# Key projections from high and low halves, mixtures without differences, and first users of loads placed later, in a hybrid convolution and RWKV-7 step

## The chip, the cores and the metric

The kernel runs on one core of one Trainium2 chip. The time is the device time of one execution in microseconds (us). Five engines work side by side and meet at semaphores: TensorE (PE in the profile; PEld is its loading of weights), VectorE (DVE), ScalarE (ACT), GpSimd (POOL) and SyncE (SP), which here issues loads. Each engine takes its instructions in the order in which they were queued: while the one at the head waits, those behind it wait too. A reader follows a wait from the engine that idles to the instruction that released it.

## What is computed

One inference step through two layers in single precision: a causal convolution layer with its MLP, then an RWKV-7 layer with its MLP, on 1040 prompt tokens (16 of them learned) and 8 decode tokens, model width 1024, 16 heads of 64. The change lies in the RWKV-7 layer:

```python
    prev = jnp.concatenate([shift_prev[:, None, :].astype(h.dtype), h[:, :-1]], axis=1)
    xx = prev - h
    xr = h + xx * x_mix[0]
    xw = h + xx * x_mix[1]
    xk = h + xx * x_mix[2]
    xv = h + xx * x_mix[3]
    xa = h + xx * x_mix[4]
    xg = h + xx * x_mix[5]
    r = (xr @ w_r).astype(f32)
    k = (xk @ w_k).astype(f32)
    v = (xv @ w_v).astype(f32)
    ...
    kk = kk / jnp.maximum(jnp.sqrt(jnp.sum(kk * kk, axis=-1, keepdims=True)), L2_EPS)
    k = k * (1.0 + (a - 1.0) * k_a.astype(f32))
    ...
    S_final, ys = lax.scan(_wkv7_step, S0.astype(f32), xs)
```

Each token is mixed with the one before it (`x_mix`), and six mixtures are projected. `_wkv7_step` is the recurrence over tokens; the kernel does it in chunks of 64 tokens, which needs the inverse of a small triangular matrix for each chunk and head.

## The kernel before

Activations lie with the model's 1024 rows as 8 tiles of 128 partitions, tokens along the free axis. The convolution layer and both MLPs go in three groups of about 350 tokens. Their products are made of halves: ScalarE rounds a weight block to the fast format (`wo_hi`, L158), GpSimd subtracts to get the rest (`wo_lo`, L165), the activations are split alike (`split`, L141 and L142), and `mm3` (L190 to L192) issues three products, high x high, low weight x high, high weight x low. A product in full precision is one call that leaves two records on TensorE.

The RWKV-7 mixer takes its 1048 tokens in four groups, counted from 0, of 272, 256, 256 and 264 columns (`mixer_in`). Each group runs a loop over p = 0 to 7, the output tiles of 128 rows. A step p projects r (`proj`, L909), then the gate and the two small matrices for decay and rate (l_g, l_w, l_a), then v, then the products for the step before (vt, nn, nm, the head sum pk at L1078), then pb (L803), which spreads the keys' norm. The key projections run one group ahead: those of group 0 stand before its loop, and the blocks of group g+1 stand at the end of the steps of group g (block p-1 in step p, and block 7 also in step 7). All r, k and v products are in full precision. Their weights come through one stream of loads (`col_stream`) into five buffers, four blocks ahead.

`prepare(g)` makes the mixtures: VectorE and GpSimd subtract (`xx`, L873), VectorE multiplies and adds (`mix`, L883). Index 2 is the key's mixture, 0 r's, 3 v's, 5 the gate's. In step p=1 the eight key mixtures of the next group are made in a row. Mixtures of the next group's gate and r follow during p=7.

PSUM has four banks in rotation for these products ("mm"), so a product waits until the reader of the fourth product before it is through: the copy of v's product to `vv` (ScalarE, L1114) is such a reader, and so is VectorE's `hl` in the MLP.

Beside this loop the recurrence (A, gg, bT, W, U, S, Y on TensorE) runs chunk by chunk; it is advanced at fill points inside the projections. The inverses (`inverses`) load `ni` and run some 30 pairs of tt and ni on VectorE (L1208, L1209). When the mixer ends, `mixer_out` splits its result into z_h and z_l (L142) and the last MLP begins; during it `decode_step` does the 8 decode tokens: four transposes and writes to memory (`d_dec`, L1426), one load `dq` (L1429) and 16 rounds on VectorE from L1444 on.

TensorE's order is that of the program. VectorE's and ScalarE's order comes from a scheduler that runs a timed model while the program is built; `tc.issue_after(x)` pins an instruction behind x on its engine, `kept_place` keeps it where the program has it, and the numbers that generators yield say how much filling work goes between two pieces. The mask `nmask` (L774) of the inverses' input is made from a loaded mask `m_ar` while the first layer's MLP runs.

Of the kernel before, what the change touches and what calls it, by code (L numbers as in the profile page):

```python
# [16 lines left out]
P = 128  # L17
# [29 lines left out]
def hybrid_step(tc, x_prompt, x_sample, state_conv, state_shift, state_wkv, meta_tokens,  # L47
# [10 lines left out]
    with ctx:  # L58
# [80 lines left out]
        def split(hi, lo, src, eng_lo):  # L139

            nc.scalar.copy(hi, src)  # L141
            return eng_lo.tensor_sub(lo, src, hi.bitcast(F32))  # L142
# [35 lines left out]

        def col_stream(cols, ahead):

            raws = {}
            for i in range(len(cols)):
                for j in range(i, min(i + ahead + 1, len(cols))):
                    if j not in raws:
                        raws[j] = load_raw(col_src(*cols[j][:2]), (KT, P), cols[j][2])
                yield blocks_of(raws.pop(i))
# [135 lines left out]
        def mlp(layer, groups, lag, eng_w, eng_h, fill=None, done=None):  # L322
# [16 lines left out]
            def inp(j, w, group):  # L339
                gn, hv, n, ah, al, rs, hid_pool = group  # L340
                if j % 2 == 0:
                    hid[gn, j // 2] = [hid_pool.tile([P, 2, cur["wide"]], F32R, name=f"h{q}{layer}{gn}_{j}", tag=f"h{q}") for q in "hl"]
                hh, hl = hid[gn, j // 2]
                ps = dense(w, (ah, al), n, f"in{layer}_{j}_{gn}", fill)
                with tc.high_priority(offset=HR):
                    s = ps[:, :n]
                    nc.vector.scalar_tensor_tensor(s, s, 0.0, rs()[:, :n], op0=ALU.max, op1=ALU.mult)  # L347
                    nc.scalar.activation(s, s, AF.Square)  # L348
                    low = split(hh[:, j % 2, :n], hl[:, j % 2, :n], s, eng_h)
                    marks.setdefault(f"hl{gn}", []).append(low.ins)  # L350
# [423 lines left out]
        nc.vector.tensor_scalar(nmask, m_ar[:, :32], par32[:, 0:1], None, op0=ALU.mult)  # L774
# [41 lines left out]

        hnp = pool(ld, "hnp", 1)
        mixp = pool(ld, "mixp", 24)
# [15 lines left out]
        prep, norm, kept, scans = {}, {}, {}, {}  # L834
# [22 lines left out]
        def prepare(g):  # L857
# [12 lines left out]
            xx = hnp.tile([P, KT, N1], F32, name=nm("xx"), tag="xx")  # L870
            for k in range(KT):
                with nullcontext() if g else tc.issue_after(marks["hl2"][k + 5]):
                    first = (nc.gpsimd if k % 3 == 2 else nc.vector).tensor_sub(xx[:, k, :npr], hx[:, k, 0:npr], hx[:, k, 1:1 + npr])  # L873
                if g and k in (0, 2):
                    kept_place(first)
                yield
            if npr < n:
                nc.vector.tensor_sub(xx[:, :, npr:n], sps, hx[:, :, 1 + npr:1 + n])
            def mix(i, k):

                t = mixp.tile([P, N1], F32, name=nm("mx", i, k), tag="mx")
                with nullcontext() if g else tc.issue_after(marks["out2"][2 * (k - KT) + 1 if i == 2 else -1]):
                    nc.vector.scalar_tensor_tensor(t[:, :n], xx[:, k, :n], vec("x_mix", i * KT + k), hx[:, k, 1:1 + n],  # L883
                                                   op0=ALU.mult, op1=ALU.add)
                return t[:, :n]
# [14 lines left out]

        def keys_of(p):
# [11 lines left out]

        def keys(g, fill):
# [4 lines left out]
            act = [mix(2, k) for k in range(KT)]  # L919
# [5 lines left out]
            for p in range(KT):  # L925
                yield
                ps = proj(next(wrkv), act, n, nm("k", p), fill)
# [7 lines left out]
            r16 = lorap.tile([P, N1], F32, name=nm("r16"), tag="lf")  # L935
# [8 lines left out]
        def mixer_in(g, tick):  # L944
# [140 lines left out]
            for p in range(KT):  # L1085
# [23 lines left out]
                for pl, t, nb, sign in zip(pls, (cum, nav), ("w0", "a0"), (0.5, -0.5)):  # L1109
                    nc.scalar.activation(t[:, :n], pl[:, :n], AF.Tanh, scale=0.5, bias=hvec(nb, p))  # L1110
                    nc.scalar.activation(t[:, :n], t[:, :n], AF.Copy, scale=sign, bias=sign)
# [35 lines left out]
                for s in segs:  # L1147
# [6 lines left out]
                    nc.vector.tensor_mul(out(2), two(wa[:, :2, :]), cols(em, s).unsqueeze(2).broadcast_to([P, s[2], 2, s[3]]))  # L1154
# [7 lines left out]
                if g < 3:  # L1162
                    if p == 0:
# [24 lines left out]
        def inverses(c, n):  # L1188
# [8 lines left out]
            group = next((g for g in range(4) if CHUNKS[g][0] > max(c, 1)), None)  # L1197
            while group and group not in scans:
# [4 lines left out]
            for j in range(top - 2, 0, -1):  # L1203
# [3 lines left out]
                with tc.issue_after(scans[group]) if group and j == top - 2 else nullcontext():  # L1207
# [207 lines left out]
        def decode_step():  # L1415

            with ExitStack() as s:
# [12 lines left out]
                yield 6  # L1430
# [149 lines left out]
        with ExitStack() as l1:  # L1580
# [15 lines left out]
            def mixer_out(g, actp, fill, add):  # L1596
# [5 lines left out]
                for p in range(0, KT, per):  # L1602
# [6 lines left out]
                    for i in range(some):  # L1609
                        split(z[0][p + i][:, :n], z[1][p + i][:, :n], v[:, i], nc.vector)  # L1610
# [72 lines left out]
            DL, DN, NL = 74, 90, 16  # L1683
# [75 lines left out]
```

## Time and profile before

| what | us |
|---|---|
| three runs | 2680.71, 2673.79, 2672.78 |
| median | 2673.79 |
| the profiled execution, its own time | 2680.24 |
| its span in the profile | 2678.5 |
| TensorE busy in it | 2602.9 (97%) |
| VectorE, ScalarE, GpSimd busy | 1725.7, 1132.7, 1450.9 |

The profiled execution took 2680.24 us, 1.7 more than the span that the page divides and 6.45 more than the median. A row of a timeline gives the start within the span, the busy time, engine, line, operation, output and inputs, and in brackets how long the engine had idled before it and what ended that. A row with x2 holds several instructions on end. In a row of clock windows stand the stretch, its length, each engine's busy time and count (PE, PEld, DVE, ACT, POOL), TensorE's granted clock as a share of full speed, the share of the DMA engines' time in use, and GB/s. Groups give the count, the total and the mean in ns.

### The profile page before, as it was taken

Reading aid. Unit: us, or ns where it says so; the run is one execution under the profiler, and the core shown is the slowest. Engines: PE = TensorE matmul, PEld = TensorE weight load, DVE = VectorE, ACT = ScalarE, POOL = GpSimd, SP = SyncE. Lnnn points to the kernel's source line nnn. Section 1 sums busy time; section 2 is a strip of 40 time slices with the busy share of each in tenths; the row PEclk is TensorE's granted clock in tenths of the full one; section 3 lists DMA queues with packets and bytes.
Section 4 is the critical chain, followed back from the end, with each engine's and each line's share of the span. In section 5 each row is a group of like instructions: output and inputs, shape, how many; then the busy total and the mean of one; then the engine's idle time right before and its main releaser. Section 6 shows DMA issues by size and latency. Waiting matters only on the chain.

```text
span 2678.5 us, 51360 instructions
## 1 busy us (share of the span) xinstructions
PE 2602.9 (97%) x19796; PEld 2450.6 (91%) x19796; DVE 1725.7 (64%) x3584; ACT 1132.7 (42%) x2097; POOL 1450.9 (54%) x2060
## 2 busy tenths in 40 slices
PE   9999999999999999999899999899999999999998
PEld 8999999999998999877777887689999999999998
DVE  6999999997445444444857567686679643344435
ACT  5546445444444333333344445545443542222223
POOL 7677878878877776122211113375578763333331
PEclk9999999999999999999999999999999999999999
DMA  6663544554456443668766867897666542222211
GB/s 188 176 168 104 167 141 132 158 177 134 142 154 183 124 138 113 201 188 211 188 181 180 206 168 193 209 211 179 156 204 176 155 131 71 64 71 71 67 52 44
DMA packets 602058, 400.20 MB, mean 149 GB/s; under 512 B 96128, under 2 KB 548928, under 8 KB 601814
## 3 DMA queue, kind: packets, MB, share of 16 engines
q1 hardware_dynamic: 573764, 360.08, 49.1%
q0 software_dynamic: 8720, 26.35, 3.1%
q10 hardware_dynamic: 19330, 10.49, 1.4%
q8 instruction: 156, 2.56, 0.4%
q14 instruction: 88, 0.72, 0.1%
HBM read 338.94 MB, written 58.83 MB: 149 GB/s over the span
## 4 chain that ended last, share of the span: by engine, by line
PE 79%; DVE 11%; DMA 3%; ACT 2%; issue 2%; POOL 2%; SPq 0%; ACTq 0%; DVEq 0%; POOLq 0%
PE out L190 8%; PE ps_in L190 8%; PE ps_in L192 8%; PE ps_in L191 8%; PE out L191 8%; PE out L192 8%; PE pk L909 4%; PE pr L909 3%; PE pv L909 2%; DVE tt L1208 1%; DVE ni L1209 1%; PE ps_g L190 1%; PE ps_o L192 1%; PE ps_g L191 1%; PE ps_g L192 1%
## 5 line engine op out<-in xcount | busy, mean ns | idle before, releaser
L165 POOL TENSOR_TENSOR wo_lo<-wo_raw,wo_hi 128x256 fp32r<-128x256 f32 x736 | 539.3, 765 | 290.0 <-ACT wo_hi L158 281.0
L165 POOL TENSOR_TENSOR wi_lo<-wi_raw,wi_hi 128x256 fp32r<-128x256 f32 x640 | 474.7, 774 | 250.5 <-ACT wi_hi L158 249.8
L190 PE MATMUL out<-hh,wo_hi 128*128 128x352 f32 (+2 forms) x1536 | 499.8, 325 | 14.9 <-DVE hl L142 10.2
L360 DVE TENSOR_TENSOR h<-h,out 128x352 f32<-128x352 f32 (+2 forms) x768 | 386.9, 512 | 169.7 <-PE out L192 168.0
L190 PE MATMUL ps_in<-m_h,wi_hi 128*128 128x352 f32 (+2 forms) x1536 | 495.3, 322 | 0.0
L192 PE MATMUL ps_in<-m_l,wi_hi 128*128 128x352 f32 (+2 forms) x1536 | 494.2, 322 | 1.1 <-DVE m_l L288 1.1
L191 PE MATMUL out<-hh,wo_lo 128*128 128x352 f32 (+2 forms) x1536 | 494.5, 322 | 0.0
L191 PE MATMUL ps_in<-m_h,wi_lo 128*128 128x352 f32 (+2 forms) x1536 | 492.9, 321 | 0.0
L192 PE MATMUL out<-hl,wo_hi 128*128 128x352 f32 (+2 forms) x1536 | 492.8, 321 | 0.0
L542 DVE SCALAR_TENSOR_TENSOR cv<-u,wdw,cv 128x348 f32<-128x348 f32 (+2 forms) x720 | 378.4, 577 | 0.7
L158 ACT CAST wi_hi<-wi_raw 128x1024 fp32r<-128x1024 f32 x160 | 167.6, 1049 | 398.1 <-PE out L192 199.0
L158 ACT CAST wo_hi<-wo_raw 128x1024 fp32r<-128x1024 f32 x184 | 192.7, 1048 | 318.3 <-PE out L192 169.9
L190 PEld LDWEIGHTS out<-hh,wo_hi 128*128 128x128 f32 x1536 | 291.0, 189 | 21.1 <-DVE hl L142 11.5
L192 PEld LDWEIGHTS ps_in<-m_l,wi_hi 128*128 128x128 f32 x1536 | 289.2, 188 | 2.6 <-DVE m_l L288 2.1
L190 PEld LDWEIGHTS ps_in<-m_h,wi_hi 128*128 128x128 f32 x1536 | 290.3, 189 | 1.4
L191 PEld LDWEIGHTS out<-hh,wo_lo 128*128 128x128 f32 x1536 | 290.1, 189 | 0.8
L191 PEld LDWEIGHTS ps_in<-m_h,wi_lo 128*128 128x128 f32 x1536 | 289.5, 188 | 0.6
L192 PEld LDWEIGHTS out<-hl,wo_hi 128*128 128x128 f32 x1536 | 289.8, 189 | 0.0
L347 DVE SCALAR_TENSOR_TENSOR ps_in<-ps_in,rs_m 128x352 f32<-128x352 f32 (+2 forms) x192 | 100.6, 525 | 258.1 <-PE ps_in L192 257.8
L142 DVE TENSOR_TENSOR hl<-ps_in,hh 128x352 fp32r<-128x352 f32 (+2 forms) x192 | 98.7, 515 | 125.2 <-ACT hh L141 125.2
L1074 POOL DMA_DIRECT2D d_n<-n x32 | 24.3, 760 | 217.5 <-DVE n L1064 112.4
L348 ACT ACTIVATE ps_in<-ps_in 128x352 f32<-128x352 f32 (+2 forms) x192 | 85.1, 444 | 125.2 <-DVE ps_in L347 124.8
(367 smaller groups left out, 4770.1 us busy)
## 6 DMA issues: line engine op xcount, KB each, us to landing
wi_raw<-in_w_mlp_in_dram SPq DMA_DIRECT2D x160, 512.0 KB
wo_raw<-in_w_mlp_out_dram SPq DMA_DIRECT2D x160, 512.0 KB
wk_raw<-in_rwkv_w_k_dram SPq DMA_DIRECT2D x32, 512.0 KB
wr_raw<-in_rwkv_w_r_dram SPq DMA_DIRECT2D x32, 512.0 KB
wv_raw<-in_rwkv_w_v_dram SPq DMA_DIRECT2D x32, 512.0 KB
d_ab<-ab POOLq DMA_DIRECT2D x32, 512.0 KB, 4.5
pg_raw<-in_conv_w_pw_dram SPq DMA_DIRECT2D x24, 512.0 KB
pa_raw<-in_conv_w_pw_dram SPq DMA_DIRECT2D x24, 512.0 KB
```

Of the source, the lines that this page charges most:

```text
L142: return eng_lo.tensor_sub(lo, src, hi.bitcast(F32))
L158: cast = nc.scalar.copy(hi[:, :a * b], raw[:, :a * b])
L165: eng_lo.tensor_sub(lo[:, cs], raw[:, cs], hi[:, cs].bitcast(F32))
L190: nc.tensor.matmul(ps, w[0], act[0], start=first, stop=False)
L191: nc.tensor.matmul(ps, w[1], act[0], start=False, stop=False)
L192: nc.tensor.matmul(ps, w[0], act[1], start=False, stop=last)
L347: nc.vector.scalar_tensor_tensor(s, s, 0.0, rs()[:, :n], op0=ALU.max, op1=ALU.mult)
L348: nc.scalar.activation(s, s, AF.Square)
L360: total = nc.vector.tensor_add(hv[:, 4 * i + m, :], hv[:, 4 * i + m, :], ps[:, :n])
L542: nc.vector.scalar_tensor_tensor(acc[m][:, :n], ug[:, m, j:j + n], wdw[:, m, j:j + 1], acc[m][:, :n], op0=ALU.mult, op1=ALU.add)
L909: nc.tensor.matmul(ps[:, :n], w[:, k, :], act[k], start=k == 0, stop=k == KT - 1)
L1208: nc.vector.tensor_mul(o, ni[:, :j, j:j + 1].broadcast_to([B, j, wd]), ni[:, j:j + 1, j + 1:top].broadcast_to([B, j, wd]))
```

## The change

1. The key projections of groups 1 to 3 become three products of halves (`proj_split`). The key mixtures are split in `halved` (ScalarE rounds, VectorE subtracts), the weight blocks in `split_block` (the same engines, 128x1024 elements). The high and low weights take two further buffers of the same five, and the stream loads three blocks ahead.
2. A mixture is x_previous * m by ScalarE, then x * (1 - m) + that by VectorE (`omix` holds 1 - m). The differences xx are gone, and so are eight of the 24 buffers.
3. The key mixtures are made after the rates of step p=1, pinned on ScalarE behind `rate` and on VectorE behind the last product of step 0 (`decayed`). `nmask` is pinned behind a later split of the MLP, the last inverses' first tt behind the last z_l, and the decode step's wait count and start (6 to 12, 90 to 96) move.
4. `em` takes the place of `cum` and is computed after the other exponentials.

```diff
+                        if cols[j][3]:
+                            halves.append((raw, *(cur["raw"].tile([P, 8 * P], F32R, name=f"{cols[j][2]}_{q}", tag="raw") for q in "hl")))
...
-        nc.vector.tensor_scalar(nmask, m_ar[:, :32], par32[:, 0:1], None, op0=ALU.mult)
+        with tc.issue_after(marks["hl2"][14]):
+            nc.vector.tensor_scalar(nmask, m_ar[:, :32], par32[:, 0:1], None, op0=ALU.mult)
...
-        mixp = pool(ld, "mixp", 24)
+        mixp = pool(ld, "mixp", 16)
+        khl = pool(ld, "khl", 1)
...
-            for k in range(KT):
-                with nullcontext() if g else tc.issue_after(marks["hl2"][k + 5]):
-                    first = (nc.gpsimd if k % 3 == 2 else nc.vector).tensor_sub(xx[:, k, :npr], hx[:, k, 0:npr], hx[:, k, 1:1 + npr])
...
+                with tc.issue_after(a_pin) if a_pin else nullcontext():
+                    nc.scalar.activation(t[:, :npr], hx[:, k, 0:npr], AF.Copy, scale=m)
...
+                with tc.issue_after(v_pin) if v_pin else nullcontext():
+                    nc.vector.scalar_tensor_tensor(t[:, :n], hx[:, k, 1:1 + n], omix[:, i * KT + k:i * KT + k + 1], t[:, :n],
                                                    op0=ALU.mult, op1=ALU.add)
...
+        def halved(t, n, name):
+            hi, lo = (khl.tile([P, N1], F32R, name=name + q, tag="k" + q, bufs=KT)[:, :n] for q in "hl")
+            nc.scalar.copy(hi, t)
+            nc.vector.tensor_sub(lo, t, hi.bitcast(F32))
+            return hi, lo
...
-        wrkv = col_stream([(w_of[s], p, f"w{s}{g}_{p}") for s, g, p in blocks_used()], 4)
+        wrkv = col_stream([(w_of[s], p, f"w{s}{g}_{p}", s == "k" and g > 0) for s, g, p in blocks_used()], 3)
+
+        def split_block():
+
+            raw, hi, lo = halves.pop(0)
+            kept_place(nc.scalar.copy(hi, raw))
+            nc.vector.tensor_sub(lo, raw, hi.bitcast(F32))
+            return blocks_of(hi), blocks_of(lo)
...
+        def proj_split(w, act, n, name, fill):
+            ps = bank(f"p{name}")
+            for k in range(KT):
+                mm3(ps[:, :n], [part[:, k, :] for part in w], [part[k] for part in act], k == 0, k == KT - 1)
...
-                if p == 1 and g < 3:
-                    for _ in coming:
-                        pass
-                    ks = carry["keys"] = keys(g + 1, both)
-                    next(ks)
...
+                if p == 1 and g < 3:
+                    for _ in coming:
+                        pass
+                    pins[g + 1] = rate.ins, decayed[g]
+                    ks = carry["keys"] = keys(g + 1, both)
+                    next(ks)
                 ps = proj(next(wrkv), act_v, n, nm("v", p), both)
...
-                em = t_("em", p)
-                nc.scalar.activation(em[:, :n], cum[:, :n], AF.Exp, scale=DECAY_SCALE)
...
+                em = cum
+                nc.scalar.activation(em[:, :n], cum[:, :n], AF.Exp, scale=DECAY_SCALE)
...
                 if g < 3:
+                    for _ in keys_of(p):
+                        w_k.append(split_block())
...
-            group = next((g for g in range(4) if CHUNKS[g][0] > max(c, 1)), None)
-            while group and group not in scans:
+            group = next((g for g in range(4) if CHUNKS[g][0] > max(c, 1)), 4)
+            while group not in scans:
                 yield 1
...
-                yield 6
+                yield 12
...
+                        _, low = split(z[0][p + i][:, :n], z[1][p + i][:, :n], v[:, i], nc.vector)
+                scans.setdefault(4, low.ins)
...
-            DL, DN, NL = 74, 90, 16
+            DL, DN, NL = 74, 96, 16
```

Where the new order stands, at three places. In these rows wa is a step's rates and keys, mx_2_k the key mixture of tile k, mk_kh its high half, wk_p_h a key block's high half.

ScalarE in step p=1 of group 0, from the rates to the copy of vv. Before:

```order
L1111 ACTIVATE wa_1_12752<-wa_1_12752 128x272 x2
L1138 ACTIVATE wa_1_12752<-wa_1_12752,omka,negs 128x272
L1125 ACTIVATE em_1_12822<-wa_1_12752 128x272
L1129 ACTIVATE ex_1_12824<-wa_1_12752 128x4x64
L1133 ACTIVATE ex_1_12824<-wa_1_12752 128x16
L1134 COPY wc<-ex_1_12824 128x4
L1136 COPY wc<-ex_1_12824 128x1
L1114 COPY vv_1_12772<-pv_1_12763 128x272
L1047 COPY vt_0_12777<-vt_0_12776 128x256
```

Now:

```order
L1139 ACTIVATE wa_1_12753<-wa_1_12753 128x272 x2
L888 ACTIVATE mx_2_0_12762<-hx_12733,pvec 128x256
L888 ACTIVATE mx_2_1_12769<-hx_12733,pvec 128x256
L1171 ACTIVATE wa_1_12753<-wa_1_12753,omka,negs 128x272
L926 CAST wk_0_h<-wk_0_raw 128x1024
L1160 ACTIVATE ex_1_12880<-wa_1_12753 128x4x64
L1164 ACTIVATE ex_1_12880<-wa_1_12753 128x16
L912 CAST mk_0h<-mx_2_0_12762 128x256
L912 CAST mk_1h<-mx_2_1_12769 128x256
L1148 COPY vv_1_12830<-pv_1_12821 128x272
L1080 COPY vt_0_12835<-vt_0_12834 128x256
L1084 COPY vm_0_12841<-vt_0_12834 16x128
```

Two products, the weights' cast and two high halves now stand between the rates and vv_1.

ScalarE in step p=7 of group 0, up to the copy of vv. Before:

```order
L1110 ACTIVATE wa_7_13488<-l_a_13490,half 128x272
L1111 ACTIVATE wa_7_13488<-wa_7_13488 128x272 x2
L1138 ACTIVATE wa_7_13488<-wa_7_13488,omka,negs 128x272
L1125 ACTIVATE em_7_13559<-wa_7_13488 128x272
L1129 ACTIVATE ex_7_13561<-wa_7_13488 128x4x64
L1133 ACTIVATE ex_7_13561<-wa_7_13488 128x16
L1134 COPY wc<-ex_7_13561 128x4
L1136 COPY wc<-ex_7_13561 128x1
L1114 COPY vv_7_13508<-pv_7_13499 128x272
```

Now (mx_0 is r's mixture of the next group):

```order
L1164 ACTIVATE ex_7_13733<-wa_7_13662 128x16
L888 ACTIVATE mx_0_2_13876<-hx_12733,pvec 128x256
L888 ACTIVATE mx_0_3_13879<-hx_12733,pvec 128x256
L1171 ACTIVATE wa_7_13662<-wa_7_13662,omka,negs 128x272
L926 CAST wk_6_h<-wk_6_raw 128x1024
L888 ACTIVATE mx_0_4_13882<-hx_12733,pvec 128x256
L1167 COPY wc<-ex_7_13733 128x4
L1166 ACTIVATE wa_7_13662<-wa_7_13662 128x272
L1169 COPY wc<-ex_7_13733 128x1
L888 ACTIVATE mx_0_5_13885<-hx_12733,pvec 128x256
L888 ACTIVATE mx_0_6_13888<-hx_12733,pvec 128x256
L1148 COPY vv_7_13682<-pv_7_13673 128x272
```

The next group's mixtures and the cast of key block 6 stand between the step's own work and vv_7.

VectorE in the last MLP, where the decode tokens' dq is first used (t from Sdec and dq). Before:

```order
L347 SCALAR_TENSOR_TENSOR ps_in_16_0_22368<-ps_in_16_0_22368,rs_m_20041 128x328
L142 TENSOR_TENSOR hl_16_22367<-ps_in_16_0_22368,hh_16_22366 128x328
L1497 TENSOR_TENSOR ebv_1_22325<-ez_1_22356,ebv_1_22325 128x512
L1498 TENSOR_TENSOR egt_1_22326<-ebv_1_22325,egt_1_22326 128x512
L347 SCALAR_TENSOR_TENSOR ps_in_17_0_22418<-ps_in_17_0_22418,rs_m_20041 128x328
L360 TENSOR_TENSOR h_0_19245<-h_0_19245,out_7_0_0_22457 128x328
L360 TENSOR_TENSOR h_0_19245<-h_0_19245,out_7_0_1_22465 128x328
L1444 TENSOR_TENSOR t_22559<-Sdec_22558,dq 128x256
L142 TENSOR_TENSOR hl_16_22367<-ps_in_17_0_22418,hh_16_22366 128x328
```

Now:

```order
L364 TENSOR_TENSOR h_0_19918<-h_0_19918,out_6_0_7_23022 128x328
L350 SCALAR_TENSOR_TENSOR ps_in_16_0_23047<-ps_in_16_0_23047,rs_m_20714 128x328
L1480 TENSOR_TENSOR t_23303<-Sdec_23302,dq 128x256
L141 TENSOR_TENSOR hl_16_23046<-ps_in_16_0_23047,hh_16_23045 128x328
L1533 TENSOR_TENSOR ebv_1_23004<-ez_1_23035,ebv_1_23004 128x512
L1481 TENSOR_REDUCE sa<-t_23303 128x4
L1482 TENSOR_TENSOR Sdec_23302<-Sdec_23302,dq 128x256
L1534 TENSOR_TENSOR egt_1_23005<-ebv_1_23004,egt_1_23005 128x512
L350 SCALAR_TENSOR_TENSOR ps_in_17_0_23093<-ps_in_17_0_23093,rs_m_20714 128x328
L1483 TENSOR_TENSOR t_23303<-sa,dq 128x256
L364 TENSOR_TENSOR h_0_19918<-h_0_19918,out_7_0_0_23132 128x328
```

The first user stood ahead of the hl of ps_in_17, and stands ahead of that of ps_in_16, one projection earlier.

More of the change, by code (lines that the diff above doesn't have):

```diff
@@ L918, in keys @@
             mix = prep[g][0]
-            act = [mix(2, k) for k in range(KT)]
+            act = [mix(2, k) for k in range(KT)] if g == 0 else list(zip(*(halved(mix(2, k, lorap, "lf", 2), n, nm("mk", k)) for k in range(KT))))
             pn = bank(nm("pn"), "x")
@@ L1206, in inverses @@
                 o = o[:, :j * wd].rearrange("p (s t) -> p s t", t=wd)
-                with tc.issue_after(scans[group]) if group and j == top - 2 else nullcontext():
+                with tc.issue_after(scans[group]) if j == top - 2 else nullcontext():
                     nc.vector.tensor_mul(o, ni[:, :j, j:j + 1].broadcast_to([B, j, wd]), ni[:, j:j + 1, j + 1:top].broadcast_to([B, j, wd]))
```

47 lines of the change are left out of this document (27 added, 20 removed).

## The prediction

> **What bounds the kernel now.** I read the page first, then TensorE's table of waits, then timelines and clock windows round each wait.
>
> ```profile
> PE 2602.9 (97%) x19796; PEld 2450.6 (91%) x19796; DVE 1725.7 (64%) x3584; ACT 1132.7 (42%) x2097; POOL 1450.9 (54%) x2060
> ```
> ```profile
> PE out L190 <- DVE hl L142: 10.2, 5, 5.4
> PE pb L803 <- ACT vv L1114: 7.0, 8, 1.7
> ...
> PE ps_oo L192 <- DVE z_l L142: 5.8, 2, 5.2
> PE l_a L1108 <- DVE rk L1121: 5.8, 1, 5.8
> ```
>
> TensorE is busy 97% of 2678.5 us, so time goes only where its own work shrinks or where one of its few waits goes. In the table (total, times, longest) three waits exceed 5 us, and in each VectorE only looks guilty. The timelines show what it stood behind: an instruction at its queue's head that waited for a load.
>
> ```profile
> 863.63 3.64 DVE L774 TENSOR_SCALAR nmask<-m_ar,par32q 128x32 f32<-128x32 f32 x1 [4.22 <-DMA m_ar<-m_ar]
> 868.03 0.66 PE L190 MATMUL out<-hh,wo_hi 128*128 128x348 f32 x1 [5.40 <-DVE hl L142]
> 1273.62 0.42 DVE L873 TENSOR_TENSOR xx<-hx 128x256 f32<-128x256 f32 x1 [7.90 <-DMA hx<-d_hn]
> 1277.10 1.22 PE L1108 MATMUL l_a<-lwa,wa 64*128 64x256 f32 x2 [5.81 <-DVE rk L1121]
> 1741.90 0.21 DVE L1208 TENSOR_TENSOR tt<-ni 128x30 f32<-128x30 f32 x1 [4.80 <-DMA ni<-d_n]
> 1743.14 0.64 PE L192 MATMUL ps_oo<-z_l,wo_hi 128*128 128x328 f32 x1 [5.19 <-DVE z_l L142]
> 1976.07 0.63 DVE L1444 TENSOR_TENSOR t<-Sdec,dq 128x256 f32<-128x256 f32 x1 [3.92 <-DMA dq<-d_dec]
> 1977.15 0.42 PE L190 MATMUL out<-hh,wo_hi 128*128 128x328 f32 x1 [2.91 <-DVE hl L142]
> ```
> ```profile
> 868.20:871.60 3.40, 3.40 (x12) 3.40 (x13) 2.35 (x6) 0.00 (x0) 0.00 (x0) 0.50 0.55 157
> 1277.80:1281.20 3.40, 3.40 (x9) 2.42 (x8) 3.09 (x14) 1.68 (x4) 0.88 (x2) 0.50 0.25 80
> 1742.00:1745.40 3.40, 2.26 (x33) 1.98 (x35) 3.40 (x7) 0.00 (x0) 2.62 (x4) 0.51 1.02 352
> 1745.40:1748.90 3.50, 3.50 (x70) 3.50 (x66) 3.29 (x12) 0.00 (x0) 0.00 (x0) 0.50 1.08 318
> ```
>
> The figure after the five engines' busy times is the granted clock. Behind each such idle it is 0.50 for one or two windows of 3.4 us, so a wait costs its idle plus half of TensorE's busy time there: 5.40 + 1.7 = 7.1 us, 5.81 + 1.7 = 7.5, 5.19 + (2.26 + 3.50)/2 = 8.1.
>
> **The change, part by part.**
>
> *The key products.* A 256-column block was 16 full-precision records. The rows for the new kind:
>
> ```profile
> 1164.11 3.45 PE pk L909 x16
> ```
> ```profile
> 1284.61 0.28 PE L803 MATMUL pb<-r16l,hspread 128*128 128x256 f32 x1
> 1284.73 3.62 PE L909 MATMUL pk<-mx,wk_raw 128*128 128x256 f32 x16
> ```
> ```profile
> 1972.12 0.31 PE L192 MATMUL out<-hl,wo_hi 128*128 128x328 f32 x1
> 1972.27 0.32 PE L190 MATMUL out<-hh,wo_hi 128*128 128x328 f32 x1
> ```
>
> Starts count, since records overlap. The only rounded record with 256 columns (r16l) is followed 0.12 us later; at 328 columns the step is 0.15 us. 24 records at 0.12 are 2.88 us against 3.45: 0.57 saved, over 24 blocks (eight with 264 columns) about 14 us. If a record kept the 0.15 us of 328 columns, 24 would be 3.6 us and cost 3.6 in all; so -14 to +4, and I take -14, the row with the same width.
>
> *The weights' splits.* Each of the 24 blocks gets a ScalarE cast of 128x1024 and a VectorE difference of that size.
>
> ```profile
> L158 ACT CAST wi_hi<-wi_raw 128x1024 fp32r<-128x1024 f32 x160 | 167.6, 1049 | 398.1 <-PE out L192 199.0
> ```
> ```profile
> 1233.43 0.39 ACT L1114 COPY vv<-pv 128x272 f32<-128x272 f32 x1 [0.52 <-PE pv L909]
> ```
> ```profile
> 1234.07 0.73 PE L1078 MATMUL pk<-rk,hsum 128*128 128x272 f32 x2
> ...
> 1236.37 3.72 PE L909 MATMUL pk<-mx,wk_raw 128*128 128x256 f32 x16 [1.33 <-DVE n L1064]
> ```
>
> The cast takes 1.05 us and stands ahead of the copy of vv, for which pk's head sum and pb wait (it frees their bank). ScalarE stood idle 0.52 us before this copy, so with the cast it comes about 0.5 us later; before, it ended 0.25 us ahead of the head sum's start. I take 0.2 us in 15 steps, +3 (0 to +8: 0.4 in 20). The difference needs about 1.2 us, an estimate from VectorE's 0.41 for 256 and 0.68 for 512 columns (rows below); VectorE has that time, being busy 64%, except at the changes of group.
>
> *The mixtures of the next group's keys (p=1).* ScalarE's x*m and cast, VectorE's sum and low half: 16 instructions on each engine, in pairs that pass back and forth. Before, eight sums in a row preceded the scan:
>
> ```profile
> 1142.05 0.75 ACT L1111 ACTIVATE wa<-wa 128x272 f32<-128x272 f32 x2
> 1142.83 0.61 ACT L1138 ACTIVATE wa<-wa,omka,negs 128x272 f32<-128x272 f32 x1
> ...
> 1146.64 0.40 ACT L1129 ACTIVATE ex<-wa 128x256 f32<-128x256 f32 x1
> ...
> 1147.28 0.38 ACT L1114 COPY vv<-pv 128x272 f32<-128x272 f32 x1
> ```
> ```profile
> 1142.38 3.26 DVE L883 SCALAR_TENSOR_TENSOR mx<-xx,pvec,hx 128x256 f32<-128x256 f32 x8
> ...
> 1150.01 0.78 DVE L1153 TENSOR_TENSOR ab<-rk,ex 128x512 f32<-128x512 f32 x2
> ```
> ```profile
> L142 DVE TENSOR_TENSOR r16l<-r,r16h x4: 405/422/442, 1124.3 to 1588.7; 128x256 fp32r<-128x256 f32 x2, 128x272 fp32r<-128x272 f32 x1, 128x264 fp32r<-128x264 f32 x1
> ```
> ```profile
> 1147.71 0.91 PE L1078 MATMUL pk<-rk,hsum 128*128 128x272 f32 x2 [1.99 <-ACT vv L1114]
> ...
> 1148.87 4.93 PE L909 MATMUL pk<-mx,wk_raw 128*128 128x256 f32 x16
> ```
> ```profile
> 1450.89 0.38 PE L803 MATMUL pb<-r16h,hspread 128*128 128x256 f32 x1 [1.52 <-ACT vv L1114]
> ```
>
> Gone are 1.99 + 1.3 us (4.93 against 3.62), 1.52, and the 7.5 us at 1277.10: 12.3 us. New: from the rates' end at 1142.80 ScalarE does two products (0.37 each, as L1111), the key factor (0.61), the cast (1.05), the exponentials (0.5) and two casts (0.75) before vv, so vv ends near 1146.8 instead of 1147.7 and block 0 can start near 1147.9. But its six other columns still need 6 x (0.41 + 0.42) = 5.0 us of VectorE, between bv, rk, wa and ab of this step (some 2.8 us): the last lies near 1155.7, and the block of 2.88 us takes about 8, so 5 us of new waits. In groups 2 and 3 the recurrence's work fills part. I take 4 us in each, clock included: +12 (2 to 7 each). Net 0 (-6 to +9). ScalarE's first product is now the first to meet hx: in group 2 that load landed at 1273.62, about when the rates end without the stall, so I cost it at nothing; each us that it lands later, vv and the key factor behind it wait. The eight differences xx a group go. With 16 buffers in place of 24, mx_0 of the first group waits for the key products that read mx_2; its eight sums (3.3 us) fit under key block 7 and the gate's product, two blocks of 3.5 us or more, so I cost that at nothing, as I do em behind ex, which only ab needs.
>
> *Changes of group (p=7).* ScalarE gets the mixtures mx_5 and mx_0 of the next group and the cast of wk_6 before vv_7. Seven products at 0.37 and the cast are 3.6 us more in front of vv_7; less the 0.52 idle it ends near 1236.8 instead of 1233.8. The head sum, at 1234.07 before, then waits 2.7 us (the 1.33 us before the key block is inside), and wk_7's cast comes behind vt, so the next block waits some 2 us more. With the clock, 4 us at each of three changes: +12 (0 to +20; the key's raw, high and low blocks take three of five buffers, so r's next load starts later too).
>
> *First users queued later.* SP's loads keep their order. nmask moves nine splits of the hidden layer back, to where m_ar has long landed: -7.1.
>
> ```profile
> 1747.48 0.68 DVE L1364 TENSOR_TENSOR fs<-S,wc 128x512 f32<-128x512 f32 x1
> ```
>
> z_l no longer stands behind the last inverses' first tt, but fs (L1364), which frees the bank for A, now does, behind three pairs of tt and ni that wait for the load of 1741.90: of 8.1 us I take 4 (0 to 8). For dq:
>
> ```profile
> 1967.32 0.31 ACTq L1426 DMA_DIRECT2D d_dec<-dst  x1
> ...
> 1971.24 0.44 ACTq L1429 DMA_DIRECT2D dq<-d_dec  x1
> ```
>
> The load starts 3.9 us after the last write and lands 4.8 us later. In the new order write, load and first user all stand one projection (3.6 us) earlier, the user ahead of ps_in_16's hl: counted from ps_in_16's start, the load lands near 7.9 us, VectorE has waited since 4.2, and ps_in_17's hl comes near 14 where TensorE wants its bank at 10. That wait stays: 0 (-4.6 to +2).
>
> **The sum**, against the profiled execution's 2680.24 us (6.45 above the median): -14 + 3 + 0 + 12 - 7.1 - 4 + 0 = -10.1. From the median 2673.79 this gives about 2663.
>
> **The clock, and a rule.** My new waits of 2 to 5 us hold about 1.5 us of half clock at six places, because 1.99 us of idle was enough:
>
> ```profile
> 1148.10:1151.50 3.40, 3.40 (x11) 2.81 (x10) 2.78 (x7) 0.00 (x0) 1.49 (x4) 0.50 0.50 126
> ```
>
> The Trainium skill (TensorE: Matmul & The Clock Gate, "HAM oscillation — how this bites in real kernels") has as its rule that TensorE must not idle for more than about 3.4 us. By that rule most of the new waits would keep the clock. The row above, 0.50 after 1.99 us, disagrees, and I go by the row.
>
> **Rivals.**
> - *The two engines keep up* at p=1 and p=7 (ScalarE is busy 42%, VectorE 64%): terms at their low ends, in part; -14 - 6 - 7 - 4 with +3 left is -28, 2646. Against: the rows show both queues in order, and the cast in front of vv. Chance 0.16.
> - *The new waits keep full clock*: 9 us less, 2654. Against: the row of 1148.10. Chance 0.08.
> - *Slower: vv behind the weights' cast.* Every key block, not six, waits for ScalarE or the low half. The rest of the change is -14 - 7.1 - 4 = -25; at 1.05 us for each of 24 blocks, the cast's whole length, that is used up. At 1.5 us it is +11: 2685. For: 8 waits for vv already; against: 0.52 us of idle before vv, and the products' 0.57. Chance 0.17.
> - *Products no cheaper than 0.144 us a record* (24 x 0.144 = 3.45): the 14 us fall away, 2677. Only one row with 256 columns speaks against. Chance 0.06.
> - *Waits for loads only move*: ScalarE's x*m now meets hx first, z_l's gain is eaten by fs: -14 + 3 + 12 - 7.1 = -6, 2668, up to 2677 if p=1 costs its 9 as well. Chance 0.07.
>
> **How the numbers follow.** My forecast has 0.46: its own range, -17 to -3, gives 2657 to 2671, and a measurement tells about 0.3% (8 us) from no change, so three quarters of it are faster, one quarter the same. Faster: 0.34 + 0.16 + 0.08 = 0.58; same: 0.12 + 0.06 + 0.07 = 0.25; slower 0.17. The range reaches to the fast rival and to the slow one: 2641 to 2686.
>
> **What the next profile would show.** Right: no idle near 868; key records 0.12 us apart; TensorE waiting in key block 0 for VectorE's low halves (p=1) and for vv at p=7; still a wait behind dq; z_l's wait gone, one for fs in its place. Wrong, if key block 0 runs without gaps or the steps of every p show a wait for vv of over 1 us.

## The result, and the profile after

The changed kernel takes 2696.11 us (median, 2695.48 to 2699.78), against 2676.97 for the kernel before in the same comparison: 1.0075 times, with a 95% interval of 1.0054 to 1.0096. It is about 20 us slower, where 10 us less was forecast. Its profiled execution has a span of 2698.1 us (2678.5 before).

The page's busy times, and the row of cores with the mean granted clock of TensorE:

```profile
PE 2613.6 (97%) x19988; PEld 2467.1 (91%) x19988; DVE 1747.6 (65%) x3608; ACT 1222.3 (45%) x2305; POOL 1445.5 (54%) x2052
```
```profile
core 0: 2698.1 us, clock 0.981
```

Of the 19.6 us that the span grew, 10.7 are busy time of TensorE (2613.6 against 2602.9) and 8.9 are idle time (84.5 against 75.6), though its products are cheaper. The clock says why the busy time grew: before, its mean was 0.991, so (1 - 0.991) x 2678.5 = 24 us of full-clock time were withheld, and now (1 - 0.981) x 2698.1 = 51. Part of that falls into idle time, where it costs nothing. So the loss is made of new waits and, no less, of the half clock round them.

TensorE's waits in the changed kernel (total, times, longest):

```profile
PE pb L808 <- ACT vv L1148: 10.0, 5, 3.5
...
PE pb L808 <- DVE n L1097: 7.5, 4, 3.1
...
PE pk L194 <- DVE wk_l L927: 5.8, 4, 2.9
PE A L1282 <- DVE fs L1400: 4.6, 1, 4.6
PE pk L193 <- ACT mk_4h L912: 4.0, 3, 2.6
...
PE pk L193 <- ACT mk_2h L912: 3.8, 3, 1.4
PE pk L195 <- DVE mk_2l L913: 3.6, 3, 1.6
```

The waits for nmask (5.4), z_l (5.2) and l_a (5.8) are gone. New are those for the key's halves (mk, wk_l), and pb waits 17.5 us for vv (ScalarE) and n (VectorE's product of nn with nmask) where it waited 7.0, all of it for vv. A wait for fs stands at A.

Where the time goes is seen from the start of the same TensorE instruction in two traces. The table gives the difference to the kernel before in us, for the changed kernel and for the runs of the next section; r(g,p) is the start of r's product in step p of group g. Each execution begins a little sooner or later, as the first row shows, so a stage is read from the step between two rows. The profiled executions are not the medians either: that of the kernel before took 2680.24 us, 3.3 more than its median of 2676.97, and that of the changed kernel 2699.78.

| place | before at | changed | em first | cast early | all four | full-precision keys | two pins |
|---|---|---|---|---|---|---|---|
| first MLP, ahead of nmask | 854.88 | +1.7 | +2.4 | +1.0 | +2.7 | +1.7 | +0.4 |
| first MLP, past nmask | 873.58 | -5.7 | -4.9 | -6.3 | -4.6 | -5.6 | -6.9 |
| r(0,1) | 1136.16 | -5.7 | -4.9 | -6.3 | -4.6 | -4.1 | -6.9 |
| r(0,3) | 1167.83 | -1.7 | -2.2 | -3.5 | -6.9 | -6.9 | -6.9 |
| r(0,7) | 1224.58 | -3.5 | -3.8 | -6.0 | -9.4 | -6.9 | -6.9 |
| r(1,0) | 1249.10 | +0.2 | +0.2 | -4.9 | -8.1 | -7.6 | -6.9 |
| r(1,1) | 1266.61 | -0.7 | -1.0 | -4.9 | -7.6 | -7.4 | -7.9 |
| r(1,3) | 1307.08 | +2.9 | +1.9 | -3.4 | -5.7 | -10.8 | -8.0 |
| r(1,7) | 1380.62 | -2.6 | -3.7 | -8.8 | -7.7 | -13.1 | -7.9 |
| r(2,0) | 1408.81 | +2.0 | +2.0 | -2.8 | -4.7 | -7.5 | -7.9 |
| r(2,1) | 1433.80 | +0.3 | +0.4 | -4.9 | -6.3 | -9.1 | -7.3 |
| r(2,3) | 1478.07 | +6.9 | +6.2 | +2.7 | -3.0 | -10.0 | -7.0 |
| r(2,7) | 1552.08 | +12.6 | +6.9 | +5.3 | -5.6 | -6.7 | -7.0 |
| r(3,0) | 1582.56 | +18.3 | +13.5 | +8.4 | -3.8 | -4.4 | -7.0 |
| mixer's output | 1735.06 | +24.0 | +13.9 | +12.7 | -3.1 | +1.5 | -8.1 |
| last MLP, past z_l | 1874.05 | +17.8 | +10.0 | +7.4 | -7.8 | -3.0 | -15.1 |
| last MLP, past dq | 1995.94 | +17.4 | +9.5 | +6.8 | -10.1 | -3.5 | -15.7 |
| end | 2678.45 | +19.6 | +11.0 | +7.3 | -8.5 | -1.4 | -16.0 |

In the changed kernel steps 1 and 2 lose 3.9, 3.6 and 6.5 us in groups 0 to 2, step 7 loses 3.6, 4.6 and 5.8, steps 3 to 6 of group 2 lose 5.7, and group 3, which has no key block, another 5.7. Steps 3 to 6 of group 0 gain 0.43 each. Steps 3 to 6 of group 1 gain 5.5 in all, more than four cheaper blocks can give; no run takes this apart.

Step p=1 of group 2 in the changed kernel: first ScalarE, then VectorE ahead of n, then TensorE, then windows.

```profile
1442.29 1.03 ACT L926 CAST wk_h<-wk_raw 128x1024 fp32r<-128x1024 f32 x1
1443.35 0.74 ACT L1341 COPY gg<-gg 32x256 f32<-32x256 f32 x2
1444.11 0.42 ACT L1160 ACTIVATE ex<-wa 128x256 f32<-128x256 f32 x1
1444.56 1.07 ACT L1352 COPY bkt<-bT 128x512 f32<-128x512 f32 x2
1445.63 1.28 ACT L1512 ACT_TABLE_LOAD   x1
1446.93 0.30 ACT L1512 ACTIVATE ems<-ems,eps_t 128x8 f32<-128x8 f32 x1
...
1447.75 0.36 ACT L1148 COPY vv<-pv 128x256 f32<-128x256 f32 x1
1448.02 0.37 ACT L1080 COPY vt<-vt 128x256 f32<-128x256 f32 x1
1448.40 1.28 ACT L1166 ACT_TABLE_LOAD   x1
```
```profile
1446.80 1.22 DVE L927 TENSOR_TENSOR wk_l<-wk_raw,wk_h 128x1024 fp32r<-128x1024 f32 x1
1447.93 0.40 DVE L1245 TENSOR_TENSOR ni<-ni,tt 128x238 f32<-128x238 f32 x1
1448.25 0.29 DVE L1097 TENSOR_TENSOR n<-nn,nmask 128x128 f32<-128x128 f32 x1
```
```profile
1448.59 0.58 PE L808 MATMUL pb<-r16h,hspread 128*128 128x256 f32 x1 [3.12 <-DVE n L1097]
...
1452.15 0.59 PE L193 MATMUL pk<-mk_2h,wk_h 128*128 128x264 f32 x1 [1.44 <-ACT mk_2h L912]
...
1455.82 0.59 PE L193 MATMUL pk<-mk_4h,wk_h 128*128 128x264 f32 x1 [0.58 <-ACT mk_4h L912]
1456.21 0.42 PE L194 MATMUL pk<-mk_4h,wk_l 128*128 128x264 f32 x1
```
```profile
1446.80:1450.20 3.40, 1.61 (x7) 1.61 (x8) 3.40 (x10) 3.36 (x10) 1.34 (x2) 0.62 0.13 39
1450.20:1453.60 3.40, 1.32 (x5) 0.70 (x3) 3.40 (x10) 2.01 (x7) 0.10 (x1) 0.50 0.69 212
1453.60:1457.00 3.40, 2.58 (x7) 1.75 (x8) 3.40 (x11) 2.48 (x7) 0.75 (x1) 0.50 0.34 118
1457.00:1460.40 3.40, 2.72 (x10) 2.11 (x10) 3.38 (x11) 1.92 (x6) 0.00 (x0) 0.50 0.11 36
1460.40:1463.80 3.40, 3.40 (x67) 2.98 (x67) 3.18 (x9) 0.87 (x3) 0.00 (x0) 0.50 0.56 169
```

The cast, the recurrence's copies and a table load stand ahead of vv, which is done at 1448.11. But the wait of 3.12 us ends last with n, at 1448.54: on VectorE the difference of the weights and an inverse (tt and ni) stand ahead of it. So an earlier vv alone would have moved nothing here. The clock falls, and key block 0 then comes in pieces. VectorE is busy 3.38 to 3.40 us of each 3.40 until 1460.40. The clock is at 0.50 in the four windows from 1450.20 on; only the last of them has TensorE busy throughout, and W, po and yn behind the block run at half rate too.

In step 3 of the same group the square root's table load and em's both stand ahead of vv:

```profile
1495.73 1.28 ACT L1512 ACT_TABLE_LOAD   x1
1497.02 0.30 ACT L1512 ACTIVATE ems<-ems,eps_t 128x8 f32<-128x8 f32 x1
1497.34 1.28 ACT L1166 ACT_TABLE_LOAD   x1
1498.63 0.42 ACT L1166 ACTIVATE wa<-wa 128x256 f32<-128x256 f32 x1
1498.96 0.18 ACT L1167 COPY wc<-ex 128x4 f32<-128x4 f32 x1
1499.04 0.36 ACT L1148 COPY vv<-pv 128x256 f32<-128x256 f32 x1
```
```profile
1499.46 0.58 PE L808 MATMUL pb<-r16h,hspread 128*128 128x256 f32 x1 [3.20 <-ACT vv L1148]
```

### The profile page after: what moved, and what is told of

Same layout as the page of the kernel before. It is cut to its first block, busy times and chain, and to the rows that moved or that the text cites. A ratio compares the mean times of both kernels' runs of the same rounds, so it can differ in the third digit from the quotient of the medians.

```text
span 2698.1 us, 52063 instructions
## 1 busy us (share of the span) xinstructions
PE 2613.6 (97%) x19988; PEld 2467.1 (91%) x19988; DVE 1747.6 (65%) x3608; ACT 1222.3 (45%) x2305; POOL 1445.5 (54%) x2052
## 4 chain that ended last, share of the span: by engine, by line
PE 82%; DVE 9%; DMA 3%; ACT 3%; issue 2%; POOL 1%; SPq 0%; ACTq 0%; DVEq 0%; POOLq 0%
PE ps_in L193 8%; PE out L193 8%; PE ps_in L194 8%; PE ps_in L195 8%; PE out L194 8%; PE out L195 8%; PE pr L933 3%; PE pv L933 2%; PE ps_g L193 1%; PE ps_o L193 1%; PE ps_o L195 1%; PE ps_oo L193 1%; PE ps_g L194 1%; PE ps_g L195 1%; PE ps_o L194 1%
## 5 line engine op out<-in xcount | busy, mean ns | idle before, releaser
L193 PE MATMUL out<-hh,wo_hi 128*128 128x352 f32 (+2 forms) x1536 | 499.3, 325 | 10.2 <-DVE h L364 8.6
```

Of the source, the lines that this page charges most:

```text
L193: nc.tensor.matmul(ps, w[0], act[0], start=first, stop=False)
```

## The experiments

Each median stands beside its ratio to the kernel before, measured on the same chip, with the 95% interval. The kernel before had medians from 2674.25 to 2677.34 us in the four sets of runs, so a difference of 3 us between runs of two sets is not settled by their medians.

**em ahead of ex.**

```diff
+                em = cum if p == 1 else lorap.tile([P, N1], F32, name=nm("em", p), tag="lf", bufs=2)
+                if p != 1:
+                    nc.scalar.activation(em[:, :n], cum[:, :n], AF.Exp, scale=DECAY_SCALE)
                 ex = pr.tile([P, 5, HS + 1], F32, name=nm("ex", p), tag="ex")
...
-                em = cum
-                nc.scalar.activation(em[:, :n], cum[:, :n], AF.Exp, scale=DECAY_SCALE)
+                if p == 1:
+                    nc.scalar.activation(em[:, :n], cum[:, :n], AF.Exp, scale=DECAY_SCALE)
```

> The changed kernel, with em again computed ahead of ex (in a buffer of the key mixtures' temporary, except at p=1), the one part that is undone. Theory A: in groups 2 and 3 the norm's square root now falls between ex and em, so ScalarE loads the exponential's table (1.28 us) once more ahead of vv; with em first the waits for vv of 1.7 to 3.5 us lose 1.3 us each and some half clock, 6 to 12 us in all: 2684 to 2690 us. Theory B: the weights' cast alone makes vv late, and the reload is hidden: 2693 to 2697 us.

2688.76 us, 1.0041 (1.0026 to 1.0055): 7.4 less than the changed kernel, theory A. By the table the gain lies where em's table load stood ahead of vv: steps 3 to 6 of group 2 lose 0.8 instead of 5.7, group 3 loses 0.5 instead of 5.7. Groups 0 and 1 hardly change. "Once more" is not what the traces show: ScalarE loads tables 43 times in the kernel before, in the changed kernel and in this run. The change moves them: before, five stood at the next step's rates (L1110) and one at em (L1125); now two stand at the rates (L1138) and five at em (L1166), four of these ahead of vv. Before, then now:

```profile
L1110 ACT ACT_TABLE_LOAD x5 | 6.4, 1283 | 2.1 <-ACT gt L1101 1.2 <-PE l_a L1108 0.9
...
L1125 ACT ACT_TABLE_LOAD x1 | 1.3, 1283 | 0.0
```
```profile
L1166 ACT ACT_TABLE_LOAD x5 | 6.4, 1283 | 0.1
...
L1138 ACT ACT_TABLE_LOAD x2 | 2.6, 1283 | 1.2 <-PE l_a L1136 0.8 <-ACT gt L1129 0.4
```

**Weights' cast early.**

```diff
-                    for _ in keys_of(p):
-                        w_k.append(split_block())
+                    if p == KT - 1:
+                        w_k.append(split_block())
...
                     for _ in keys_of(p):
                         next(ks, None)
+                    if p < KT - 1:
+                        w_k.append(split_block())
```

> The changed kernel, with the weight block of the next step split right after the present key block (ScalarE idle there) and not ahead of vv; block 7 stays. Theory A (both the cast and the reload count): each wait for vv loses about 1.05 us, and the wait of block 6 for its low half goes: 8 to 14 us less, 2682 to 2688 us. Theory B (the pairs of halves at p=1 carry the loss): 0 to 3 us less, 2693 to 2697 us. Theory C (the cast is all): 16 us less, 2680 us or under.

2687.38 us, 1.0040 (1.0025 to 1.0055): 8.7 less, theory A. Steps 3 to 6 of group 0 gain 0.62 each instead of 0.43, and the change from group 0 to 1 loses 1.1 instead of 3.6. The edit moves the cast (ScalarE) and the difference (VectorE) together, so it doesn't tell which of them cost what.

**Both.** The two edits together.

> The changed kernel with em ahead of ex and the next step's weight split behind the present key block, both edits of the first two runs. Theory A (the two lie one behind the other in ScalarE's queue ahead of vv, so they add): -7 - 9 = -16, 2679 to 2682 us. Theory B (either alone brings vv in time, the second gains nothing): 2686 to 2688 us.

2682.58 us, 1.0027 (1.0017 to 1.0038): 13.5 less than the changed kernel, where the two alone give 7.4 and 8.7. They nearly add (theory A, missed by 0.6); the result is still 20 us above what was forecast for the change.

**Key block 0 in step 2.**

```diff
-            return [p - 1] * (p > 0) + [p] * (p == KT - 1)
+            return [0] * (p == 2) + [p - 1] * (p > 1) + [p] * (p == KT - 1)
```

> The changed kernel with key block 0 moved from the end of step p=1 to that of p=2 (ahead of block 1); the mixtures and their halves are still made at p=1. Theory A (what costs at p=1 is that the pairs have no lead over their products): the gaps inside block 0, some 4 us a group and their half clock, go; step 2 gets a wait for the second weight split of 2 to 3 us: 6 to 12 us less, 2684 to 2690 us. Theory B (VectorE's and ScalarE's work itself is in the way of the step's own chain): 2693 to 2698 us.

2696.39 us, 1.0071 (1.0050 to 1.0092): no gain, theory A falls for this edit alone. The gaps in block 0 for the key's halves are gone but for one of 0.9 us, but the wait for weight halves grew from 5.8 us to 16.0:

```profile
PE pk L194 <- DVE wk_l L927: 16.0, 9, 4.3
PE pb L808 <- ACT vv L1148: 12.7, 6, 3.7
```

Two blocks at the end of one step need two splits. In group 1 the buffers hold the second one up: ScalarE stands idle 1.72 us before the second cast until the first difference is done, and VectorE 0.51 before the second difference until products of block 0 are. In groups 0 and 2 the second difference stands behind VectorE's other work instead.

**Mixtures behind vv at p=7.**

```diff
-                nc.scalar.copy(vv[:, :n], ps[:, :n])
+                last_vv[g] = nc.scalar.copy(vv[:, :n], ps[:, :n]).ins
...
+                if g and i in (0, 5):
+                    a_pin = last_vv[g - 1]
```

> The changed kernel with ScalarE's part of the next group's gate and r mixtures queued behind the copy of vv of p=7. Theory A (these products make vv late at the change of group): three changes of group lose 2 to 3 us each, 2687 to 2690 us. Theory B (the weight split of blocks 6 and 7 sets the time there, or the gate's product now waits for its mixtures): 2694 to 2698 us.

2697.00 us, 1.0078 (1.0061 to 1.0095): no gain, theory B. The products were not what set the time: the wait for wk_l is 8.8 us instead of 5.8.

**All four.** Block 0's weights are split at the end of step 1, block 1's in step 2 ahead of both blocks.

> All four: em first, weights' cast early, key block 0 in step 2, mixtures behind vv. Theory A (the change's loss is only order on ScalarE ahead of vv and lead at p=1): the gains add to about 33 us, 2660 to 2668 us, below the kernel before by 8 to 16. Theory B (the splits' work on VectorE keeps half of it): 2672 to 2682 us.

2670.37 us, 0.9980 (0.9968 to 0.9991): 25.7 less than the changed kernel, between the theories, nearer B. The two edits that gain nothing alone give 12 us once em is first and the casts are early. What is left:

```profile
PE pk L194 <- DVE wk_l L930: 11.7, 6, 2.8
...
PE pb L808 <- ACT vv L1151: 7.9, 6, 4.0
```

Six waits for the low half of a second block (steps 2 and 7 of three groups) take 11.7 us, most of what the products save.

**Full-precision keys.** The splits taken out, the mixtures and first users left as changed. The mixtures have 24 buffers again, and the weights' stream has no halves.

```diff
-            act = [mix(2, k) for k in range(KT)] if g == 0 else list(zip(*(halved(mix(2, k, lorap, "lf", 2), n, nm("mk", k)) for k in range(KT))))
+            act = [mix(2, k) for k in range(KT)]
...
-                ps = proj_split(w_k.pop(0), act, n, nm("k", p), fill) if g else proj(w, act, n, nm("k", p), fill)
+                ps = proj(next(wrkv), act, n, nm("k", p), fill)
...
-                    for _ in keys_of(p):
-                        w_k.append(split_block())
```

> The changed kernel with the key projections in full precision: no cast, no halves, 24 buffers of mixtures, the rest as changed. Theory A (the splits cost more than the 14 us that the products save): nmask (-7.3), z_l (-6), hx (-7) stay gained, em's reload stays lost: 2660 to 2672 us. Rival (the mixtures on ScalarE carry the loss, the products pay for themselves): 2690 us or more.

2674.89 us, 0.9990 (0.9979 to 1.0001): 21 less than the changed kernel, so the splits, with the buffers that they take, cost some 35 us against about 14 that the products save. It is 3 us over the range of theory A. The wait for n belongs to the mixtures' new order and not to the splits, for it is nearly as long here (2.87 us in step 1 of group 2):

```profile
PE pb L808 <- DVE n L1096: 6.6, 3, 2.9
```

**Full-precision keys and em ahead of ex.**

```diff
-                em = cum
+                em = t_("em", p)
```

(moved ahead of ex as above).

> The kernel of the run with full-precision keys, with em ahead of ex besides (a tile of its own). It holds the mixtures on ScalarE, the pins and nothing else of the change. Theory A (em's place costs what the waits for vv in groups 2 and 3 show, 8 to 10 us): 2664 to 2668 us. Theory B (without the casts ScalarE has time for the reload): 2672 to 2676 us.

2670.93 us, 0.9981 (0.9971 to 0.9990): 4 us for em, between the theories. In this run's trace group 3 still loses 4.6 us with em first (from -10.5 at r(3,0) to -5.9 at the mixer's output). By the trace ScalarE stands idle there for 2.91 us until a load (sv) lands, ahead of the rates of step 5, and pb then waits 3.6 us for vv.

**The same, and the mixtures behind vv.**

> The same with ScalarE's part of the next group's gate and r mixtures behind the copy of vv of p=7. Theory A (with full-precision keys no weight split waits behind them, so vv is on time and the three changes of group lose 1 to 3 us each): 3 to 6 us below the run before, 2659 to 2664 us. Theory B (as in the changed kernel, the wait moves to the next reader): equal to it within 2 us.

2667.49 us, 0.9962 (0.9948 to 0.9976): 3.4 less, theory A by the difference; the range named with it is missed by 3 us. The edit that gained nothing with the splits behind it gains without them.

**Two pins in the kernel before.** nmask behind `marks["hl2"][14]` and the last inverses behind the last z_l, as in the change's diff, nothing else.

> The kernel before, with nmask queued behind a later split and the last inverses' first tt behind the last z_l, nothing else. Theory A: the two waits at 868 and 1743 go as in the changed kernel's trace, 7.3 and about 6 us: 2662 to 2666 us. Rival: what they free is lost further on (the wait for fs at A): 2669 to 2672 us.

2666.41 us, 0.9964 (0.9952 to 0.9976): 10.2 less than before, at the edge of theory A. In the table nmask gives 7.3 (from +0.4 to -6.9) and z_l 7.0 (from -8.1 to -15.1). The table's last row, -16.0, is more than the medians give, since the profiled execution of the kernel before took 3.6 us more than its median in this set and that of this run 2.2 less. The wait for l_a stays, and one for fs comes:

```profile
PE pb L804 <- ACT vv L1115: 7.8, 8, 2.2
PE l_a L1109 <- DVE rk L1122: 6.2, 1, 6.2
...
PE A L1247 <- DVE fs L1365: 5.1, 2, 3.5
```

**Two pins and the decode step's numbers.**

```diff
-                yield 6
+                yield 12
...
-            DL, DN, NL = 74, 90, 16
+            DL, DN, NL = 74, 96, 16
```

> The kernel before with the two pins (nmask, last inverses) and the decode step's numbers of the change (wait count 12, start 96). Theory A (the first user of dq moves ahead together with its load, so VectorE waits for it as before): within 2 us of the run with the two pins alone, 2664 to 2669 us. Theory B (the wait of 2.91 us and its half clock go): 2661 to 2663 us.

2666.28 us, 0.9961 (0.9947 to 0.9976): no difference, theory A. VectorE still waits for dq's load, here and in the changed kernel, and TensorE's wait behind it is one for h in place of that for hl (2.34 us against 2.91). First this run, then VectorE and TensorE in the changed kernel:

```profile
1957.70 1.02 DVE L1445 TENSOR_TENSOR t<-Sdec,dq 128x256 f32<-128x256 f32 x1 [2.75 <-DMA dq<-d_dec]
```
```profile
1987.28 0.99 DVE L1480 TENSOR_TENSOR t<-Sdec,dq 128x256 f32<-128x256 f32 x1 [2.78 <-DMA dq<-d_dec]
```
```profile
1992.60 0.42 PE L193 MATMUL out<-hh,wo_hi 128*128 128x328 f32 x1 [2.34 <-DVE h L364]
```

**Two pins, and the differences queued later.** The mixtures stay on VectorE; only the differences of a later group wait for the last product of step 0.

```diff
-                with nullcontext() if g else tc.issue_after(marks["hl2"][k + 5]):
+                with tc.issue_after(decayed[g - 1] if g else marks["hl2"][k + 5]) if g == 0 or k % 3 != 2 else nullcontext():
                     first = (nc.gpsimd if k % 3 == 2 else nc.vector).tensor_sub(xx[:, k, :npr], hx[:, k, 0:npr], hx[:, k, 1:1 + npr])
```

> The kernel before with the two pins (nmask, last inverses) and, besides, VectorE's first differences xx of each later group queued behind the last product of step 0, as the change pins its mixtures; mixtures, keys and em as before. Theory A (the wait for hx at 1273 is one of order on VectorE alone and needs no mixture on ScalarE): the 5.81 us and their half clock go, 5 to 7 us below the run with the two pins: 2659 to 2662 us. Theory B (the differences come later, and with them the scan, the key mixtures or vv at p=1): 2665 us or more.

2663.46 us, 0.9954 (0.9938 to 0.9970). This is the lowest median of all, and 0.46% below the kernel before. The wait for l_a is gone from its table. The waits for vv stay about as long as in the run with two pins, and one for an inverse's tt is new:

```profile
PE pb L804 <- ACT vv L1115: 8.2, 8, 3.1
...
PE pb L804 <- DVE tt L1210: 2.2, 1, 2.2
```

So theory A holds for the place, since the wait goes; the price is not shown. The median lies between the theories' ranges, 3 us below the run with two pins, but it is 10.8 us below its own kernel before where that run is 10.2 below its own. In the traces, counted from the row ahead of nmask, this run is nearly 6 us ahead of the run with two pins at the mixer's output and only 0.9 at the end; what takes the rest back in the last MLP stays open.

## Why the prediction was wrong

**nmask: right.** -7.1 forecast, -7.3 in the changed kernel from the row ahead of it to the row past it, and the same in the run with two pins. The waits before held a fourth of over 5 us that the prediction passed over, 5.3 us for the first load of the prompt (tx); the change doesn't touch it.

**The key products: right in themselves.** 0.57 us a block was forecast. Block 1 of group 0 takes 2.93 us in the changed kernel (1162.74 to the next product at 1165.67) where it took 3.45, and with the casts early steps 3 to 6 of group 0 gain 0.62 each. Over 24 blocks that is 12 to 15 us.

**vv behind the weights' cast in the usual steps: right for group 0, wrong for group 2.** The prediction had 0.2 us a step, from a ScalarE that idles 0.52 us there. In group 0 it was 0.19 (0.62 less 0.43). In group 2 the recurrence's copies and the table loads fill that idle, as the rows of step 3 show, so the row of group 0 was no measure for it.

**em behind ex, costed at nothing: wrong.** I asked who needs em, not what the move does to ScalarE's function tables. The norm's square root now falls between ex and em, and table loads of 1.28 us that stood at the next step's rates now stand at em, in four places ahead of vv (one before). Undone, it gives 7.4 us, and in the table 5.2 of the 5.7 us that group 3 loses, for which the prediction had no term.

**Step p=1: wrong in size.** The removal was right: the wait for l_a is gone, and v's product in step 1 of group 1 starts 7.0 us sooner against the kernel before than the step's r. The new waits were put at 12 us with 1.5 us of clock in each. Steps 1 and 2 lose 3.9 + 3.6 + 6.5 = 14.0 us although six cheaper blocks lie in them (-3.4) and 12.3 us of waits went, so the new waits and their half clock are near 30, if all that was counted as gone went. With full-precision keys the same steps gain 2.9, 3.4 and 0.9 = 7.2, so about 5 of the 30 belong to the mixtures' new order and some 25 to the splits. The forecast's own list of instructions was right for group 0: vv, then six columns in pieces until 1150.6, 9.1 us after the block's start. What was missed is the clock, which stays at half for 6.8, 13.7 and 17.1 us in groups 0 to 2, and that in group 2 VectorE runs an inverse at the same time. The stretches at half clock:

```profile
1147.26:1154.08 6.82, 6.54 (x20) 5.43 (x21) 2.46 (x6) 2.76 (x7) 1.48 (x2) 0.50 0.56 169
1280.38:1294.03 13.65, 9.06 (x35) 7.01 (x36) 10.91 (x36) 4.59 (x11) 0.75 (x1) 0.50 0.56 171
1447.63:1464.69 17.06, 12.52 (x95) 10.05 (x96) 16.79 (x48) 10.45 (x28) 2.19 (x4) 0.50 0.42 130
```

Half of TensorE's busy time in them, (6.54 + 9.06 + 12.52)/2 = 14 us, is the price of the clock, where three times 1.5 us were forecast.

**Change of group: under-sized.** 12 forecast; 3.6 + 4.6 + 5.8 = 14.0 measured with six cheaper blocks inside, so about 17. The cause named first, the mixtures ahead of vv, is not the one that sets it while the splits are there (the run with them behind vv gains nothing). The second, the late low half of the next block, holds 2.9, 1.1 and 1.0 us of idle at the three changes; pb's wait for n, which the prediction did not name, holds another 1.3 and 2.7 at the second and third, and no run takes it apart.

**z_l: right, a little better.** -4 forecast, -6.2 between the mixer's output and 1874; the wait for fs at A (4.6 us) came in its place as said.

**dq: right.** No gain was forecast; the load and its first user moved together, and VectorE's wait stayed.

**The rivals.** The one on the slower side had a part of the mechanism, ScalarE's queue ahead of vv, and a price of 2685, 11 us short. It was given 0.17, because it was thought to need every key block. Its sign, a wait for vv of over 1 us in the steps of every p, did not come: pb waits for vv five times in all. The terms for steps 1, 7 and the rest were sized by rows of group 0, which has none of the recurrence's work beside it. The shortfall of the sum is 30 us: 18 at p=1, 5 at p=7, 10 for em by the table (4.9 in group 2, 5.2 in group 3), with smaller terms of both signs between. The growth of the withheld clock, from 24 to 51 us, runs through all of these.

**The clock rule.** The prediction weighed the Trainium skill's "HAM oscillation" section of TensorE: Matmul & The Clock Gate, which asks for no idle over about 3.4 us, against a row with 1.99 us. In the window ahead of that row, from 1144.70 to 1148.10, TensorE was busy 1.41 us of 3.40. The new rows go further the same way: no single idle in key block 0 of group 2 is over 1.44 us, 3.12 us stand ahead of it, and the clock is 0.50 over four windows of 3.4 us in which TensorE was busy 1.32 to 3.40 us.

What stays open: whether more buffers for halves would let the products pay. It was not tried.

## What to carry to other kernels

A cheaper product that needs its operands split is only as cheap as the place where the split stands: here about 14 us saved on TensorE cost some 35 in waits and half clock, because the splits stood in the queues of ScalarE and VectorE ahead of what TensorE waits for. When an instruction moves on an engine, list what else falls between it and its neighbours, and which loads of function tables move with it, and size the wait in the fullest stage, not the emptiest. First users of late loads are worth pinning by themselves: two such pins and nothing else gave 0.36% (0.24% to 0.48%); a third took its wait away, but no clear time.

## What the runs showed of the hardware

Half rate lasts while work comes in pieces: in the rows from 1450.20 to 1460.40 TensorE was busy 39%, 76% and 80% of three stretches of 3.4 us at 0.50, and the next stretch was at 0.50 each time. The window after them, with TensorE busy 3.40 of 3.40 us, was the last one wholly at 0.50. So such work can run at half rate for much longer than its gaps add up to: 17.1 us here, for gaps of 3.12, 1.44, 0.75, 0.58 and 0.57 us. I had expected a penalty of one window for each gap.

A function's table load took ScalarE 1.28 us each time. Moving one exponential behind another added no load (43 in each of the three traces), but it put loads ahead of vv in four places, and undoing that gave 7.4 us.
